# Writing each group of split weights at its own offset of 0 to 112 bytes inside the SBUF buffers

## The chip, the cores and the metric

One core of one Trainium2 chip runs the kernel. The metric is the device time in microseconds (us) of one execution; several executions are made and the median is compared.

## The reference

A trunk of two layers on 256 tokens of width 1024, in float32. Each layer is a half-step SwiGLU feed-forward block, a token-mixing block and a second feed-forward block, each followed by a layer norm:

```python
x = layer_norm(ALPHA * x + 0.5 * swiglu(x, ffn1_gate, ffn1_up, ffn1_down), ln1_g, ln1_b)
proj = x @ w_in                       # 1024 -> 2328 columns, for three mixers
mix = concat([short_conv(...), gmlp_spatial(...), nsa_attention(...)]) @ w_out
x = layer_norm(ALPHA * x + mix, ln2_g, ln2_b)
x = layer_norm(ALPHA * x + 0.5 * swiglu(x, ffn2_gate, ffn2_up, ffn2_down), ln3_g, ln3_b)

def swiglu(x, w_gate, w_up, w_down):  # 1024 -> 2816 -> 1024
    return (silu(x @ w_gate) * (x @ w_up)) @ w_down
```

## The kernel before

**Products in three passes.** Every large product is made of float32r matmuls. A float32 matrix is split in two float32r matrices, `hi` (the value rounded) and `lo` (what is left), and a product is hi*hi + hi*lo + lo*hi. So each pair of tiles costs three matmuls, each with a weight load of its own (in the trace PE is the matmul row of TensorE and PEld its weight loads).

**The stream of weights.** `_plan` lists all weight blocks in the order of their use. `ensure` walks through the list: it loads a block of at most 1024 columns into a `raw` buffer (SP's queue, L159), ScalarE rounds it into a `hi` buffer (L162) and VectorE subtracts to get the `lo` buffer (L163). There are 5 raw, 12 hi and 12 lo buffers, used in turn; a buffer is written again once the matmuls that read it are done. `blocks` and `kslices` hand out the tiles of a group and call `ensure` six or seven blocks ahead. A group is all blocks with the same key: the gate, up or down weights of one chunk of the feed-forward block, or one column group of `w_in`. `index` holds the keys in order: 71 per layer, 142 in all.

**Three kinds of large product.** The operand that is loaded into the array is called stationary here, the one that streams through is called moving.

- Channel products (`proj_chan`, L195 to L197): stationary is a 128x128 piece of a weight buffer, moving are 256 columns of the transposed activations `xTh` or `xTl`. The gates and ups of chunks 1 to 9 (tiles `pg`, `pu`) and most of the input projection (`pc`) are made so.
- Token products (`mm3`, L185 to L187): stationary is a 128x128 piece of `xTh` or `xTl`, moving is the weight buffer, 512 columns in the gate and up of chunk 0 (`pg`, `pu`), 280 or 256 columns in the first two groups of the input projection (`pt`).
- Down and output products (also `mm3`): stationary is a piece of the hidden activations (`hTh`, `hTl`) or of the mixers' output (`mixh`, `mixl`), moving are 512 columns of the weight buffer (`y`, `yo`).

**Where the operands lie.** A buffer has one address, the same in all 128 partitions; it is counted in bytes here. In the built program the raw, hi and lo buffers begin at 43328, 63808 and 112960, and each next buffer of a kind lies 4096 bytes further. All of them begin 64 bytes after a multiple of 128. So do the buffers of `hTh`, `hTl`, and of `mixh`, `mixl` (which are taken from the hi and lo buffers). `xTh` (25472) and `xTl` (33664) begin at a multiple of 128. The pieces that the matmuls of 128, 256 and 512 columns take begin at multiples of 512 bytes from there, so they have the same place in a stretch of 128 bytes as the buffer; only the 280-column products take pieces at 0, 1120 and 2240 bytes.

The lines of the helper that all products of 512 and 280 columns go through, and of the channel products:

```python
            PE.matmul(o, lhsT=a[0], rhs=b[0], start=start, stop=False)         # L185
            PE.matmul(o, lhsT=a[0], rhs=b[1], start=False, stop=False)         # L186
            return PE.matmul(o, lhsT=a[1], rhs=b[0], start=False, stop=stop)   # L187
...
                    PE.matmul(p[:, b, :], lhsT=hi, rhs=xTh[:, k, :], start=k == 0, stop=False)       # L195
                    PE.matmul(p[:, b, :], lhsT=hi, rhs=xTl[:, k, :], start=False, stop=False)        # L196
                    PE.matmul(p[:, b, :], lhsT=lo, rhs=xTh[:, k, :], start=False, stop=k == KC - 1)  # L197
```

Of the kernel before, what the change touches and what calls it, by code (L numbers as in the profile page):

```python
# [8 lines left out]
F32R = mybir.dt.float32r  # L9
# [112 lines left out]
def _build(tc, A, out):  # L122
# [3 lines left out]
    with ExitStack() as es:  # L126
# [3 lines left out]
        hip = pool("hi", 12)  # L130
        lop = pool("lo", 12)
# [7 lines left out]
        index = {}  # L139
# [9 lines left out]
        def ensure(i):  # L149
            while len(loaded) <= min(i, len(plan) - 1):  # L150
                key, k, n, split, o = plan[len(loaded)]
                src = A["ws"][o:o + 128 * n].rearrange("(p c) -> p c", p=128)
                if not split:
                    raw = (hip, lop)[k % 2].tile([128, n], F32, name="w1", tag=("hi", "lo")[k % 2])
                    SP.dma_start(raw, src)
                    loaded.append((raw, None))
                    continue
                raw = rawp.tile([128, n], F32, name="raw", tag="raw")
                stream.append(SP.dma_start(raw, src))  # L159
                hi = hip.tile([128, n], F32R, name="hi", tag="hi")  # L160
                lo = lop.tile([128, n], F32R, name="lo", tag="lo")
                splits.append((ACT.copy(hi, raw),  # L162
                               DVE.tensor_tensor(lo, raw, hi.bitcast(F32), ALU.subtract)))  # L163
                loaded.append((hi, lo))

        def blocks(key, ahead=None):
            if ahead is None:
                ahead = 7 if len(key) == 4 else 6
            ids = index[key]
            ensure(ids[-1] + ahead)  # L170
            return [loaded[i] for i in ids]
# [56 lines left out]
        for h, n in ((0, 1), (1, 4)):  # L228
            with ExitStack() as order:
                for i in prev:  # L230
                    order.enter_context(tc.issue_after(i.ins))
                x_load(0, h)
                prev = to_xT(0, h)
            with ExitStack() as order:
                for i in prev:
                    order.enter_context(tc.issue_after(i.ins))
                ensure(n)
            prev = splits[-1]
        for h in range(2):
            x_load(1, h)  # L240
        ensure(7)

        def second_x(products):
# [554 lines left out]
```

## Time and profile before

| | us |
|---|---|
| median of 3 runs (993.42 to 995.68) | 993.79 |
| the profiled execution, its own time | 993.1 |
| its span, first to last instruction | 991.4 |
| PE busy in the span | 978.0 |
| PEld (weight loads) busy | 887.4 |
| DVE (VectorE) busy | 603.2 |
| ACT (ScalarE) busy | 468.4 |

The profiled execution lies 0.7 us below the median. Busy time counts an instruction from its start to its end; matmuls overlap, so the time that one matmul costs is the distance from its start to the start of the next, called the spacing here, and not its own duration. The profile gives the spacing by the start times of the timeline, or by the number of matmuls in a stretch.

### The profile page before, as it was taken

How to read it: one execution, taken by the hardware profiler on the slowest of the kernel's cores; microseconds unless marked ns; L12 is line 12 of the kernel's file. 1: busy time of each engine (PE TensorE's matmuls, PEld its weight loads, DVE VectorE, ACT ScalarE, POOL GpSimd, SP SyncE). 2: the span in 40 equal slices, each digit the busy share in tenths (PEclk: the TensorE clock that was granted, in tenths of full speed). 3: DMA queues.
4: the chain of work that ended last, by engine and by line, in shares of the span. 5: the costliest groups of instructions: out<-in, count | busy, mean ns of one | idle time of the engine just before them, and what ended most of it. 6: DMA issues, size and time to landing. Idle time of an engine off the chain costs nothing.

```text
span 991.4 us, 16634 instructions
## 1 busy us (share of the span) xinstructions
PE 978.0 (99%) x6824; PEld 887.4 (90%) x6828; DVE 603.2 (61%) x830; ACT 468.4 (47%) x658; POOL 19.7 (2%) x42
## 2 busy tenths in 40 slices
PE   7999999999999999999999999999999999999996
PEld 6999999899878899999889999998988789999995
DVE  6655455686769555455584545548678785545534
ACT  6644444256655444344354444434565663534420
POOL 1000000010000000000000000000000000000000
PEclk9999999999999999999999999999999999999998
DMA  8967565385226666556375766554642265755601
GB/s 284 331 241 237 171 198 187 105 309 160 87 86 194 231 213 194 189 189 205 94 231 195 255 205 202 196 157 168 237 149 85 86 229 198 253 190 184 205 16 42
DMA packets 53067, 183.17 MB, mean 185 GB/s; under 512 B 6656, under 2 KB 7168, under 8 KB 52992
## 3 DMA queue, kind: packets, MB, share of 16 engines
q1 hardware_dynamic: 52992, 182.12, 55.2%
q8 instruction: 53, 0.87, 0.4%
q14 instruction: 22, 0.18, 0.1%
HBM read 181.05 MB, written 1.05 MB: 184 GB/s over the span
## 4 chain that ended last, share of the span: by engine, by line
PE 99%; DMA 0%; DVE 0%; issue 0%; SPq 0%; DVEq 0%; ACT 0%
PE y L185 8%; PE y L187 8%; PE y L186 8%; PE pu L195 7%; PE pg L195 7%; PE pg L197 7%; PE pu L197 7%; PE pg L196 7%; PE pu L196 7%; PE pc L195 3%; PE pc L197 3%; PE pc L196 3%; PE pg L187 2%; PE yo L187 2%; PE yo L185 2%; PE pg L185 2%
## 5 line engine op out<-in xcount | busy, mean ns | idle before, releaser
L163 DVE TENSOR_TENSOR lo<-raw,hi 128x1024 fp32r<-128x1024 f32 (+2 forms) x326 | 389.9, 1203 | 283.1 <-ACT hi L162 267.3
L162 ACT CAST hi<-raw 128x1024 fp32r<-128x1024 f32 (+2 forms) x326 | 335.1, 1037 | 385.6 <-PE pu L196 153.6
L195 PE MATMUL pu<-xTh,hi 128*128 128x256 f32 x576 | 161.3, 280 | 0.0
L195 PE MATMUL pg<-xTh,hi 128*128 128x256 f32 x576 | 161.3, 280 | 0.0
L197 PE MATMUL pu<-xTh,lo 128*128 128x256 f32 x576 | 160.8, 279 | 0.0
L197 PE MATMUL pg<-xTh,lo 128*128 128x256 f32 x576 | 160.8, 279 | 0.0
L196 PE MATMUL pu<-xTl,hi 128*128 128x256 f32 x576 | 160.8, 279 | 0.0
L196 PE MATMUL pg<-xTl,hi 128*128 128x256 f32 x576 | 160.7, 279 | 0.0
L185 PE MATMUL y<-hi,hTh 128*128 128x512 f32 x352 | 138.6, 394 | 0.0
L187 PE MATMUL y<-hi,hTl 128*128 128x512 f32 x352 | 137.4, 390 | 0.0
L186 PE MATMUL y<-lo,hTh 128*128 128x512 f32 x352 | 136.9, 389 | 0.0
L195 PEld LDWEIGHTS pu<-xTh,hi 128*128 128x128 f32 x576 | 108.1, 188 | 1.1
L196 PEld LDWEIGHTS pu<-xTl,hi 128*128 128x128 f32 x576 | 107.8, 187 | 1.1
L197 PEld LDWEIGHTS pu<-xTh,lo 128*128 128x128 f32 x576 | 108.3, 188 | 0.0
L197 PEld LDWEIGHTS pg<-xTh,lo 128*128 128x128 f32 x576 | 108.3, 188 | 0.0
L195 PEld LDWEIGHTS pg<-xTh,hi 128*128 128x128 f32 x576 | 108.1, 188 | 0.1
L196 PEld LDWEIGHTS pg<-xTl,hi 128*128 128x128 f32 x576 | 107.8, 187 | 0.1
L187 PEld LDWEIGHTS y<-hi,hTl 128*128 128x128 f32 x352 | 66.0, 188 | 14.7
L186 PEld LDWEIGHTS y<-lo,hTh 128*128 128x128 f32 x352 | 66.1, 188 | 12.6
L185 PEld LDWEIGHTS y<-hi,hTh 128*128 128x128 f32 x352 | 66.1, 188 | 12.3
L195 PE MATMUL pc<-xTh,hi 128*128 128x256 f32 x256 | 73.0, 285 | 0.0
L197 PE MATMUL pc<-xTh,lo 128*128 128x256 f32 x256 | 72.5, 283 | 0.0
(153 smaller groups left out, 1246.4 us busy)
## 6 DMA issues: line engine op xcount, KB each, us to landing
raw<-in_ws SPq DMA_DIRECT2D x312, 512.0 KB, 4.6
w<-in_ws SPq DMA_DIRECT2D x8, 512.0 KB, 6.1
lng<-in_ln SPq DMA_DIRECT2D x6, 512.0 KB, 6.7
lnb<-in_ln SPq DMA_DIRECT2D x6, 512.0 KB, 7.5
raw<-in_ws SPq DMA_DIRECT2D x8, 256.0 KB, 4.0
raw<-in_ws SPq DMA_DIRECT2D x4, 420.0 KB, 3.5
x<-in_x SPq DMA_DIRECT2D x4, 256.0 KB, 4.5
out<-x SPq DMA_DIRECT2D x4, 256.0 KB, 2.1
```

Source lines behind the costliest of these rows:

```text
L162: splits.append((ACT.copy(hi, raw), DVE.tensor_tensor(lo, raw, hi.bitcast(F32), ALU.subtract)))
L163: DVE.tensor_tensor(lo, raw, hi.bitcast(F32), ALU.subtract)))
L185: PE.matmul(o, lhsT=a[0], rhs=b[0], start=start, stop=False)
L186: PE.matmul(o, lhsT=a[0], rhs=b[1], start=False, stop=False)
L187: return PE.matmul(o, lhsT=a[1], rhs=b[0], start=False, stop=stop)
L195: PE.matmul(p[:, b, :], lhsT=hi, rhs=xTh[:, k, :], start=k == 0, stop=False)
L196: PE.matmul(p[:, b, :], lhsT=hi, rhs=xTl[:, k, :], start=False, stop=False)
L197: PE.matmul(p[:, b, :], lhsT=lo, rhs=xTh[:, k, :], start=False, stop=k == KC - 1)
```

## The change

Each group gets a number, its place in the list of keys modulo 8. The group's hi and lo parts are written into their buffers 4 elements (16 bytes) times that number behind the buffer's begin. To make room each hi and lo buffer grows from 1024 to 1056 elements, 4096 to 4224 bytes.

```diff
-                hi = hip.tile([128, n], F32R, name="hi", tag="hi")
-                lo = lop.tile([128, n], F32R, name="lo", tag="lo")
+                at = 4 * (list(index).index(key) % 8)
+                hi = hip.tile([128, 1056], F32R, name="hi", tag="hi")[:, at:at + n]
+                lo = lop.tile([128, 1056], F32R, name="lo", tag="lo")[:, at:at + n]
```

Everything that reads `hi` and `lo` goes through these slices. The other tiles that are taken from the same buffers (`KH`, `KL`, `QS`, `mixh`, `mixl`, the tile `w1`) stay at the buffer's begin, and the raw buffers are as before. In the built program the hi buffers now begin at 63808 and every 4224 bytes after it, the lo buffers at 114496 and every 4224; all still 64 bytes after a multiple of 128. The tiles allocated behind them move up by 3072 bytes, which is 24 times 128. `xTh` and `xTl` stay. The instructions of all five engines, their order, their shapes and what they wait for are the same in the two built programs. Of the 72 groups of channel products in the feed-forward blocks 8 have the number 0, and 8 to 11 each other number; of the 40 down groups 4 have the number 0.

## Rows read from the trace of the kernel before

**Rows 1.** The page: span, busy share of the engines, granted clock by fortieths, chain.
```profile
span 991.4 us, 16634 instructions
...
PE 978.0 (99%) x6824; PEld 887.4 (90%) x6828; DVE 603.2 (61%) x830; ACT 468.4 (47%) x658; POOL 19.7 (2%) x42
...
PEclk9999999999999999999999999999999999999998
...
PE 99%; DMA 0%; DVE 0%; issue 0%; SPq 0%; DVEq 0%; ACT 0%
```

**Rows 2.** Groups of PE, shapes apart: busy us, mean ns of one.
```profile
L195 PE MATMUL pu<-xTh,hi 128*128 128x256 f32 x576 | 161.3, 280 | 0.0
...
L185 PE MATMUL y<-hi,hTh 128*128 128x512 f32 x352 | 138.6, 394 | 0.0
...
L195 PE MATMUL pc<-xTh,hi 128*128 128x256 f32 x256 | 73.0, 285 | 0.0
...
L185 PE MATMUL yo<-hi,mixh 128*128 128x512 f32 x64 | 26.5, 414 | 0.0
L185 PE MATMUL pg<-hi,xTh 128*128 128x512 f32 x64 | 26.2, 409 | 0.0
```

**Rows 3.** Busy time by stretch: from:to, length, busy (instructions) of each engine, clock, DMA.
```profile
156.04:161.69 5.65, 5.65 (x50) 5.65 (x49) 2.45 (x3) 2.59 (x3) 0.00 (x0) 1.00 0.47 141
714.46:720.11 5.65, 5.65 (x50) 5.65 (x49) 4.55 (x6) 5.33 (x7) 0.00 (x0) 1.00 0.25 82
226.81:232.25 5.44, 5.44 (x51) 5.44 (x50) 4.35 (x6) 5.12 (x7) 0.00 (x0) 1.00 0.21 59
175.76:189.36 13.60, 13.60 (x62) 11.26 (x60) 6.00 (x11) 0.00 (x0) 0.92 (x1) 1.00 0.15 47
321.27:326.17 4.90, 4.90 (x23) 3.93 (x22) 2.74 (x3) 2.61 (x3) 0.00 (x0) 1.00 0.38 111
345.00:350.00 5.00, 5.00 (x45) 5.00 (x44) 0.11 (x1) 1.05 (x1) 0.00 (x0) 1.00 0.02 8
```

**Rows 4.** The same view for `pc` on PE alone: stretches with the closer spacing, and all.
```profile
208.70:237.70 29.00, 27.95 (x240) 1.00 0.66 221
696.14:707.10 10.96, 10.96 (x96) 1.00 0.89 313
0.00:991.40 991.40, 98.72 (x768) 1.00 0.56 185
```

**Rows 5.** Timeline of PE: L185 of four successive 280-column triples (start, duration).
```profile
202.84 0.29 PE L185 MATMUL pt<-hi,xTh 128*128 128x280 f32 x1
...
203.22 0.29 PE L185 MATMUL pt<-hi,xTh 128*128 128x280 f32 x1
...
203.62 0.29 PE L185 MATMUL pt<-hi,xTh 128*128 128x280 f32 x1
...
204.00 0.29 PE L185 MATMUL pt<-hi,xTh 128*128 128x280 f32 x1
```

**Rows 6.** Groups of DVE and ACT: the splits, and the shifted convolution taps.
```profile
L163 DVE TENSOR_TENSOR lo<-raw,hi 128x1024 fp32r<-128x1024 f32 x312 | 379.1, 1222 | 271.6 <-ACT hi L162 255.7 <-DMA w<-in_w 11.3
...
L478 DVE SCALAR_TENSOR_TENSOR vg<-vg,rs,gln 128x256 f32<-128x256 f32 x4 | 1.9, 481 | 0.9 <-POOL rs L302 0.9
L596 DVE SCALAR_TENSOR_TENSOR yc<-z,taps,yc 128x254 f32<-128x254 f32 x4 | 1.9, 480 | 0.1
```

**Rows 7.** Groups of ACT: the rounding of the weights.
```profile
L162 ACT CAST hi<-raw 128x1024 fp32r<-128x1024 f32 x312 | 325.5, 1052 | 373.3 <-PE pu L196 153.6 <-PE pg L196 78.5 <-PE y L187 54.7
```

**Rows 8.** Busy time by stretch, DVE alone, in the attention of the first layer.
```profile
242.00:275.00 33.00, 26.56 (x76) 1.00 0.30 97
275.00:309.00 34.00, 27.04 (x59) 1.00 0.35 104
```

## The prediction

> **What bounds the kernel now.** I read the page first. PE is busy for 978.0 of 991.4 us, the chain that ended last is PE to 99%, and the granted clock is at full speed in all slices but the last [rows 1]. So nothing but the pace of the matmuls sets the time, and the question about any change is whether it alters that pace or makes PE wait. The groups by line give counts and durations: a channel product of 256 columns lasts 280 ns, a down product of 512 columns 394 ns [rows 2]. They overlap, so these are not what one costs.
>
> For the cost I took the busy time by stretch, with stretches that run from the start of one L195 or L185 to the start of another, so that the code gives the number of products in them; the counts in the row are two or three higher, since they include matmuls that had begun before the stretch. The reader is to see four paces [rows 3]:
>
> - Channel products in the feed-forward block: 48 in 5.65 us, 117.7 ns each.
> - The same channel products in the input projection (`ks` and the first half of `q`): in the second layer, from 714.46, 48 in 5.65 us, 117.7 ns; in the first, from 226.81, 48 in 5.44 us, 113.3 ns.
> - Down products: 60 in 13.60 us, 226.7 ns, exactly twice 113.3.
> - Token products of 512 columns: 21 in 4.90 us, 233.3 ns.
>
> So a product of the same width has two paces, a close one (113.3 for 256 columns, 226.7 for 512) and a wide one (117.7 and 233.3). It is not other engines that make the difference: from 345 to 350 DVE is busy for 0.11 us, ACT for 1.05 us, the DMA share is 0.02, and about 43 channel products are still made in 5 us, at the wide pace [rows 3]. It isn't the granted clock either, which is 1.00 in all these rows. What is left is PE itself: the reading of the moving operand, and of the stationary operand of the next product, which goes on beside it. In the down products, at the close pace, both operands begin 64 bytes after a multiple of 128. In the token products one begins at 0 and the other at 64, in the channel products also, and there the wide pace rules. That fits a collision of the two reads that depends on where the operands lie. But place is not all: in the input projection of the first layer the channel products run close with the same places.
>
> **The change part by part.** No instruction is added, removed or moved on any engine, SP's queue of loads included. What changes are addresses, and with them three things.
>
> First, the writes of ACT and DVE into shifted buffers (L162, L163). Their prices are 1052 and 1222 ns per 1024 columns [rows 6, 7]. The nearest rows for a shift are the convolution taps: an operation with operands shifted by 4 and 8 bytes and 254 columns takes 480 ns, the like one without a shift and with 256 columns 481 [rows 6]. I take nothing. Were it a tenth more, it would be hidden: ACT is idle for 373.3 us before these roundings, most of it waiting for PE to free a buffer [rows 7], so the splits run ahead of their use. The cover is thinnest in the attention, where DVE is busy for 26.56 of 33 us and 27.04 of 34 [rows 8]; 6 to 7 us are free in each, and a tenth of the splits there, about twenty, would be 2.4 us. So between 0 and nothing that shows.
>
> Second, the place of the weights against the activations, which by the reading above chooses the pace. I count what can move:
>
> - Channel products at the wide pace: 6 groups of 576 in the feed-forward blocks [rows 2] are 3456; of the 768 of the input projection 240 and 96 lie in the close stretches [rows 4], so 432 are wide. Together 3888, each with 117.7 less 113.3, 4.4 ns, to gain: 17.1 us at most.
> - Token products of 512 columns: 6 groups of 64 [rows 2], 384, with 233.3 less 226.7, 6.6 ns: 2.5 us to gain at most.
> - Down and output products: 3 times 352 and 3 times 64 [rows 2], 1248, now close, with 6.6 ns to lose: 8.2 us at most.
>
> A group with the number 0 stays as it is, so seven eighths of these. No row shows a shift of 16, 32 or 48 bytes between the operands. The ends are therefore that all shifted groups are wide, and that all are close. I take the middle, that half of the new places give the close pace and half the wide one, for this reason: of the two relations that the rows show (0 and 64 bytes apart), one is close throughout and the other nearly always wide, so neither end has the rows on its side. That gives 7/8 of (-8.6 - 1.3 + 4.1), which is -5.1 us.
>
> Third, a moving operand that does not begin on a round place may be read more slowly in itself. The nearest rows are the 280-column products, whose pieces begin 64, 32 and 0 bytes after a multiple of 128: their triples take 0.38, 0.40 and 0.38 us [rows 5]. So at most 4%, on one of them. The down, output and token products are 1248 and 384 with some 228 ns, 372 us together; 4% of that on seven eighths is +13 us. I take 0, since the same place comes again later in the projection without standing out, and keep 13 for the range.
>
> **Sum.** 993.1 - 5.1 is 988.0 us for an execution like the profiled one, and as that lay 0.7 us below the median, 988.7 for the median, which I round to 989.
>
> **The rivals.**
>
> *The place does not matter.* The two paces may be set by how the stream of matmuls was entered, not by addresses: the same code with the same places runs at 113.3 in one layer and 117.7 in the other [rows 3], and it changes after small matmuls stand between. Against it: down and token products are the same helper, the same width, the same hi, lo, hi order, and differ in the stationary operand alone, and each keeps its pace throughout. Time: 993.8, within 2 us.
> The Trainium skill bears on this one: "TensorE: Matmul & The Clock Gate", in its section on what each phase is for, has two independent read ports in PE, one for each operand, so that loading the next weights takes no bandwidth from the running matmul; by that rule no place could matter and the sum would be 0. The trace agrees in that PE's pace is the same with all other engines at rest; that there are two paces for one width it doesn't explain, and so I leave it the smaller chance.
>
> *The down products lose and the gates don't gain.* This is the one on the other side. Down products have the close pace because their operands stand alike; every shift breaks that. If only the relation of 0 bytes is close, all shifted down and output products go to 233.3 ns, +7.2 us (7/8 of 8.2), while the channel products, of which only a group with the number 4 would come to stand alike, gain an eighth of 17.1, 2.1 us, or nothing if their pace is set by how they were entered. Time: 999 to 1001. It decides from the point where the share of down products that go wide is more than 2.4 times the share of channel and token products that go close (19.6 against 8.2 us). For it: 0 bytes is the one relation that is close in all its rows. Against it: a collision that needs the two reads to meet should be the exception among eight places.
>
> *Reading from a shifted place is slow in itself*, the third item above: up to +13 us, 1006.8; it decides if the cost is over 1.5% of the 372 us. For it is the one triple of 0.40 us [rows 5], against it that the others at that place differ little.
>
> *Nearly every shift is close*: 7/8 of -19.6, -17.2 us, 976.6. For it is the same thought about collisions; it is the far end of the forecast and shares its chance.
>
> That the change would not do what it says can be left out: the built program has the slices at the new addresses, and all readers use them.
>
> **How the numbers follow.** A measurement of this kernel tells about 0.2%, 2 us, from no change. The forecast with its far end (faster by 2 to 17 us) gets 0.45; no matter of place, or gains and losses that cancel, 0.23; the loss of the down products 0.20 and slow reading 0.12, together 0.32 for slower. The sum rests on a middle that no row shows, so the forecast's own range is wide, 977 to 991.7. The whole range goes from 976, all shifts close, to 1004, which takes in the loss of all down products and a part of the slow reading.
>
> **What would show it.** Right: in the profile after, stretches of channel products of different groups have different paces by their number, many at 113 ns, and some down groups are at 233; the mean durations of the L195 to L197 groups of `pg` and `pu` fall from 280 towards 276, those of `y` rise. No matter of place: all rows keep their counts and means. The loss of the down products: `y` rises with `pg`, `pu` unchanged. Slow reading: `y` and the 512-column `pg` beyond 234 ns. Wrong in another way: PE shows idle time before L185 or L195 with DVE or ACT as the releaser, or the DVE and ACT means of L162, L163 rise by tens of ns.

## The result, and the profile after

The changed kernel takes 1001.8 us (median of 4 runs, 1000.19 to 1002.69), the kernel before 993.93 in the same comparison. The ratio is 1.0077, with a 95% interval of 1.0059 to 1.0094. The change makes the kernel slower, where a gain of 5 us was forecast. The profiled execution took 1001.12 us, 999.4 of them its span. (L162, L163, L185 to L187 and L195 to L197 of before are L163, L164, L186 to L188 and L196 to L198 now.)

The page of the changed kernel: span, busy time, granted clock, the chain, and the PE groups that answer to [rows 1, 2].

```profile
span 999.4 us, 16638 instructions
...
PE 985.9 (99%) x6828; PEld 891.1 (89%) x6828; DVE 603.2 (60%) x830; ACT 468.0 (47%) x658; POOL 19.3 (2%) x42
...
PEclk9999999999999999999999999999999999999999
...
PE 98%; DMA 0%; DVE 0%; SPq 0%; issue 0%; DVEq 0%; ACT 0%
...
L196 PE MATMUL pg<-xTh,hi 128*128 128x256 f32 x576 | 161.7, 281 | 0.0
...
L186 PE MATMUL y<-hi,hTh 128*128 128x512 f32 x352 | 139.7, 397 | 0.0
```

Its groups with the shapes apart: the splits on DVE and ACT, as [rows 6, 7], and further groups of PE, as [rows 2].

```profile
L164 DVE TENSOR_TENSOR lo<-raw,hi 128x1024 fp32r<-128x1024 f32 x312 | 378.8, 1222 | 276.4 <-ACT hi L163 275.3
...
L163 ACT CAST hi<-raw 128x1024 fp32r<-128x1024 f32 x312 | 325.0, 1050 | 378.1 <-PE pu L197 160.9 <-PE pg L197 82.3 <-PE y L188 57.0
...
L196 PE MATMUL pc<-xTh,hi 128*128 128x256 f32 x256 | 73.7, 288 | 0.0
...
L186 PE MATMUL pg<-hi,xTh 128*128 128x512 f32 x64 | 25.9, 405 | 0.0
```

PE is busy 7.9 us longer and the span is 8.0 us longer; what PE idles, 999.4 less 985.9, is 13.5 us, and was 13.4. So no wait was added: the matmuls themselves go at another pace, at the full clock. The writes kept their means, 1222 and 1050 ns. The durations say where the time is only roughly: 281 for 280 ns in the gates, 397 for 394 in `y`, 288 for 285 in `pc`, 405 for 409 in the token products. The cost is read from the spacing again.

Busy time by stretch of the changed kernel, PE alone (from:to, length, busy and count, clock, DMA share, GB/s). Each of the first six stretches holds 48 channel products of one group, the seventh 78 down products, the last 24 token products. The groups' numbers are 0, 0, 0, 4, 5 and 6.

```profile
114.73:120.22 5.49, 5.49 (x49) 1.00 0.66 226
406.62:412.08 5.46, 5.46 (x51) 1.00 0.47 162
151.35:156.96 5.61, 5.61 (x51) 1.00 0.69 227
168.27:173.98 5.71, 5.71 (x50) 1.00 0.68 208
389.68:395.38 5.70, 5.70 (x50) 1.00 0.49 142
145.69:151.35 5.66, 5.66 (x49) 1.00 0.85 287
173.98:192.09 18.11, 18.11 (x81) 1.00 0.19 59
311.91:317.50 5.59, 5.59 (x26) 1.00 0.89 301
```

The paces now differ by the group's number. The number 0 has 114.4, 113.8 and 116.9 ns, so it is close for a part of its products; but the number 4, whose weights stand like `xTh` modulo 128 (both begins leave the same rest), has 119.0, the number 5 118.8, and the number 6 117.9. Before, such a stretch took 117.7 [rows 3]. The down products have 232.2 ns, for 226.7 before [rows 3]. The token products, 232.9, are nearly as they were.

The same over the whole execution, each spacing taken from the start times and summed: the channel products of the feed-forward blocks (3456) took 407.2 us before and 408.5 now, `pc` 94.2 and 95.9, the token products 92.4 and 91.8, `y` 241.4 and 246.1, `yo` 48.2 and 48.5, and the 256-column `pt` took 0.2 us more. That is +1.3, +1.7, -0.6, +4.7, +0.3 and +0.2, before rounding together 7.7 of the 7.9 us by which PE is longer busy. By number, and without the few spacings above 150 ns, the channel products have 115.6 (0), 117.7, 117.5, 119.0, 119.1 (4), 118.5, 119.4 and 118.0 ns (7). The 119.4 of the number 6 comes mostly from one group, in which 28 of the 48 products are 130 to 134 ns apart. Its busy time by stretch, PE alone:

```profile
844.71:850.82 6.11, 6.11 (x51) 1.00 0.61 186
```

That is 127.3 ns for a channel product, at the full clock. e3, below, has the same spacings in the same group. `y`, without spacings above 245 ns, has 231.7 to 233.4 in all numbers, and that holds for the number 0 as well (232.1), which the change was to leave as it is.

That last number calls for a second cause: the growth of the buffers. Before, all hi and lo buffers begin 64 bytes after a multiple of 256. With 4224 bytes from one to the next every second one begins 192 bytes after it. (The built programs mostly take the buffers in turn, but not always, so that successive blocks mostly alternate between the two places.) The prediction looked at places modulo 128 only, where this can't be seen.

### The profile page after: what moved, and what is told of

It reads as the page before. It is cut to its first block, busy times and chain, and to the rows that moved or that the text cites. A ratio compares the mean times of both kernels' runs of the same rounds, so it can differ in the third digit from the quotient of the medians.

```text
span 999.4 us, 16638 instructions
## 1 busy us (share of the span) xinstructions
PE 985.9 (99%) x6828; PEld 891.1 (89%) x6828; DVE 603.2 (60%) x830; ACT 468.0 (47%) x658; POOL 19.3 (2%) x42
## 4 chain that ended last, share of the span: by engine, by line
PE 98%; DMA 0%; DVE 0%; SPq 0%; issue 0%; DVEq 0%; ACT 0%
PE y L188 8%; PE y L187 8%; PE y L186 8%; PE pu L196 7%; PE pg L197 7%; PE pu L198 7%; PE pu L197 7%; PE pg L198 7%; PE pg L196 7%; PE pc L196 3%; PE pc L198 3%; PE pc L197 3%; PE yo L187 2%; PE yo L186 2%; PE yo L188 2%; PE pg L187 2%
## 5 line engine op out<-in xcount | busy, mean ns | idle before, releaser
L164 DVE TENSOR_TENSOR lo<-raw,hi 128x1024 fp32r<-128x1024 f32 (+2 forms) x326 | 389.7, 1203 | 288.0 <-ACT hi L163 286.8
L163 ACT CAST hi<-raw 128x1024 fp32r<-128x1024 f32 (+2 forms) x326 | 334.6, 1035 | 390.4 <-PE pu L197 160.9
L196 PE MATMUL pg<-xTh,hi 128*128 128x256 f32 x576 | 161.7, 281 | 0.0
L198 PE MATMUL pu<-xTh,lo 128*128 128x256 f32 x576 | 161.7, 281 | 0.0
L197 PE MATMUL pg<-xTl,hi 128*128 128x256 f32 x576 | 161.7, 281 | 0.0
L197 PE MATMUL pu<-xTl,hi 128*128 128x256 f32 x576 | 161.6, 281 | 0.0
L196 PE MATMUL pu<-xTh,hi 128*128 128x256 f32 x576 | 161.6, 281 | 0.0
L198 PE MATMUL pg<-xTh,lo 128*128 128x256 f32 x576 | 161.6, 281 | 0.0
L186 PE MATMUL y<-hi,hTh 128*128 128x512 f32 x352 | 139.7, 397 | 0.0
L188 PE MATMUL y<-hi,hTl 128*128 128x512 f32 x352 | 139.0, 395 | 0.0
L187 PE MATMUL y<-lo,hTh 128*128 128x512 f32 x352 | 138.8, 394 | 0.0
L196 PEld LDWEIGHTS pu<-xTh,hi 128*128 128x128 f32 x576 | 108.5, 188 | 1.3
L197 PEld LDWEIGHTS pu<-xTl,hi 128*128 128x128 f32 x576 | 108.4, 188 | 1.2
L197 PEld LDWEIGHTS pg<-xTl,hi 128*128 128x128 f32 x576 | 108.5, 188 | 0.1
L196 PEld LDWEIGHTS pg<-xTh,hi 128*128 128x128 f32 x576 | 108.5, 188 | 0.1
L198 PEld LDWEIGHTS pg<-xTh,lo 128*128 128x128 f32 x576 | 108.6, 188 | 0.0
L198 PEld LDWEIGHTS pu<-xTh,lo 128*128 128x128 f32 x576 | 108.6, 188 | 0.0
L188 PEld LDWEIGHTS y<-hi,hTl 128*128 128x128 f32 x352 | 66.1, 188 | 15.6
L187 PEld LDWEIGHTS y<-lo,hTh 128*128 128x128 f32 x352 | 66.2, 188 | 14.1
L186 PEld LDWEIGHTS y<-hi,hTh 128*128 128x128 f32 x352 | 66.2, 188 | 13.9
L196 PE MATMUL pc<-xTh,hi 128*128 128x256 f32 x256 | 73.7, 288 | 0.0
L198 PE MATMUL pc<-xTh,lo 128*128 128x256 f32 x256 | 73.1, 286 | 0.0
```

Of the source, the lines that this page charges most:

```text
L163: splits.append((ACT.copy(hi, raw), DVE.tensor_tensor(lo, raw, hi.bitcast(F32), ALU.subtract)))
```

## The experiments

The theories are told in the quoted expectations. A minus in a diff marks a line of the changed kernel; e4 to e7 start from the kernel before, and e12 from e11. The ratios are to the kernel before in the same comparison. The table gives for each kernel its median, and the mean spacing in ns of the channel products in the feed-forward blocks, of the token products without spacings over 245 ns, and of `y`, all from the start times of the profiled execution.

| kernel | us | channel | token | y |
|---|---|---|---|---|
| before | 993.93 | 117.8 | 233.4 | 228.8 |
| the change | 1001.8 | 118.2 | 232.0 | 233.3 |
| e1 bigger buffers alone | 986.97 | 115.1 | 231.4 | 231.8 |
| e2 offsets for moving weights only | 985.03 | 114.3 | 232.0 | 233.2 |
| e3 offsets for stationary weights only | 999.52 | 118.2 | 231.4 | 231.6 |
| e4 all moved by 64 bytes | 1001.69 | 120.0 | 227.6 | 228.5 |
| e5 all moved by 128 | 990.7 | 117.6 | 229.7 | 227.8 |
| e6 all moved by 256 | 994.27 | 117.8 | 233.3 | 228.8 |
| e7 all moved by 32 | 990.84 | 116.7 | 233.2 | 228.4 |
| e8 buffers of 4352 bytes alone | 994.04 | 117.8 | 233.3 | 228.8 |
| e9 these, with the change's offsets | 1000.11 | 118.1 | 233.2 | 232.2 |
| e10 these, offsets for stationary only | 997.72 | 118.5 | 233.3 | 228.8 |
| e11 these, every second block 128 further | 980.15 | 114.1 | 233.3 | 228.6 |
| e12 as e11, token weights 64 further | 977.92 | 114.1 | 227.8 | 228.6 |

### The two parts of the change (e1, e2, e3)

e1 keeps the bigger buffers and drops the offsets:

```diff
-                at = 4 * (list(index).index(key) % 8)
+                at = 0
```

> Buffers of 1056 elements (4224 bytes) as in the change, but every group at the buffer's begin. Theory A (the place of the weights within a stretch of 128 bytes decides; the offsets are the cause): as before, 994 us within 2, down products at 227 to 228 ns, channel products at 117.8. Theory B (the distance of 4224 bytes from buffer to buffer is the cause, as it ends the common place of all buffers within 512 and 1024 bytes): down products at 231 to 233 ns (+4.5 us), channel products at about 115.6 ns as the groups of number 0 have in the changed kernel (-7.6 us), 989 to 993 us.

e2 keeps the offsets of those weights that are the moving operand (down and output weights, chunk 0, the first two groups of the input projection), e3 those of the others:

```diff
+                moves = key[1] in ('kvg', 'v', 'wo') or len(key) == 4 and (key[2] == 'd' or key[3] == 0)
-                at = 4 * (list(index).index(key) % 8)
+                at = 4 * (list(index).index(key) % 8) * moves
```

In e3 the last factor is `(not moves)`.

> Offsets only for the groups whose weights are the moving operand (down, output projection, chunk 0, first two of the input projection); the others at the buffer's begin, all buffers of 4224 bytes. Theory A: down products 232 to 233 ns, channel products 117.8 as before, 999 to 1000 us. Theory B: down products 232 to 233 ns, channel products about 115.6 ns, 990 to 994 us.

> Offsets only for the groups whose weights are the stationary operand (channel products); down and token groups at the buffer's begin, all buffers of 4224 bytes. Theory A: down products 227 to 228 ns, channel products 118.0 to 118.2, 995 to 996 us. Theory B: down products 231 to 232 ns, channel products 118.0 to 118.2, 1000 to 1001 us.

Measured: e1 986.97 us, ratio 0.9932 [0.9915, 0.9949]; e2 985.03, 0.9911 [0.9895, 0.9928]; e3 999.52, 1.0058 [1.0040, 1.0076].

The bigger buffers alone, which no term of the prediction held, make the kernel 6.6 us faster. The offsets of the stationary weights then cost 12.6 us (e3 against e1) or 16.8 (the change against e2); those of the moving weights gain 1.9 us (e2 against e1), but not in the products that they move: `y` goes from 231.8 to 233.2 ns, the channel products from 115.1 to 114.3. So the change is a gain that it gives away twice over. Both e1 and e2 lie below the range that either theory gave them. What e1 does to the two kinds of product stands in its busy time by stretch, PE alone: two successive groups of 48 channel products, 48 of the second feed-forward block, and 78 down products.

```profile
45.35:50.95 5.60, 5.60 (x49) 1.00 0.82 300
50.95:56.39 5.44, 5.44 (x50) 1.00 0.53 123
343.65:349.31 5.66, 5.66 (x50) 1.00 0.04 12
171.91:189.96 18.05, 18.05 (x81) 1.00 0.18 59
```

These are 116.7, 113.3 and 117.9 ns for a channel product, with no offset anywhere, and 231.4 for a down product, where before had 226.7. In the first group the first 36 products go at 118 and the last twelve at 113.4, and the close pace stays until the next down products. In the built program the blocks of the first two groups alternate between 64 and 192 bytes; in the third group all weights lie at 64, and it stays wide.

### All weights moved against the activations (e4 to e7)

A small tile behind `xTl` moves everything that is allocated after it, all weight buffers and the hidden activations among it, against `xTh` and `xTl`, in the kernel before. Nothing else changes:

```diff
         xTl = cst.tile([128, KC, S], F32R, name="xTl")
+        cst.tile([128, 16], F32, name="pad")
```

16 elements are 64 bytes (e4), 32 are 128 (e5), 64 are 256 (e6), 8 are 32 (e7). In e4 weights and `xTh` stand alike modulo 256, both at 128; the two operands of `y` stand alike in all four.

> The kernel before, with 64 bytes left free behind the transposed activations, so that all weight buffers and the hidden activations move by 64 bytes together and stand like the transposed activations within 512 bytes; buffers 4096 bytes apart. Theory A, with the equal place as the close one: down products stay at 227 to 228 ns, channel products go from 117.8 to 113.3 and token products from 233.3 to 226.7, 975 to 977 us. Rival, after the rows of the changed kernel in which the channel operands stand a multiple of 128 bytes apart (118.6 to 119.6 ns): channel products at about 119.5 ns, +6 us, 1000 us. If places don't matter at all: 994 us.

Measured: e4 1001.69 us, ratio 1.0077 [1.0059, 1.0096]. Its busy time by stretch, PE alone: 48 channel products, 36 down products, 48 token products.

```profile
49.28:55.04 5.76, 5.76 (x50) 1.00 0.58 162
55.04:63.23 8.19, 8.19 (x38) 1.00 0.97 321
20.55:31.44 10.89, 10.89 (x50) 1.00 0.97 334
```

The token products went from 233.3 to 226.9 ns in this stretch, as the prediction's reading (standing alike is close) wants it. The channel products did the opposite, 120.0 ns, the widest mean of the table, and constant. The same relation of places gives the close pace for 512 columns and one wider than any of before for 256. This run alone refutes the step by which the prediction carried the rule from `y` to the gates; and it shows that the place decides, since nothing but addresses differs from before and 8 us are lost. For 512 columns it is the place of one operand against the other: `y` keeps 227.8 to 228.8 ns in e4 to e7, where both of its operands move together.

> The kernel before with 128 bytes left free behind the transposed activations: weights and hidden activations move together, buffers 4096 bytes apart, the stationary weights still 64 bytes off within 128 but 448 instead of 64 bytes off within 512. Theory C (the place within 256 or 512 bytes chooses between the close and the wide pace; in the kernel with buffers of 4224 bytes and no offsets the distances other than 64 ran at 113.3 to 115): channel products at 113.3 to 115, down products stay at 227 to 228, 976 to 983 us. Theory D (only the place within 128 bytes counts, and the wide pace of the kernel before comes from all its buffers standing alike): channel products at 117.8, 993 to 994 us.

> The same with 256 bytes: 320 instead of 64 bytes off within 512, equal to before within 256. Theory C with 512 bytes as the measure: 113.3 to 115 ns, 976 to 983 us; with 256 bytes as the measure, and theory D: 117.8 ns, 993 to 994 us. Down products at 227 to 228 ns in each case.

> The same with 32 bytes: every stationary weight 32 bytes nearer, as in the groups with the number 2 of the changed kernel, but alike for all buffers. If the distance from 64 modulo 128 is what costs the channel products: about 117.5 ns as those groups have, 992 to 994 us, and it may not have a close state at all; if it is the mixture of places that costs, 113.3, 976. Down products at 227 to 228 ns.

Measured: e5 990.7 us, ratio 0.9957 [0.9940, 0.9973]; e6 994.27, 0.9995 [0.9986, 1.0005]; e7 990.84, 0.9960 [0.9945, 0.9975].

A shift by 256 bytes changes neither the time nor, by more than 0.1 ns, a spacing of the table, one by 128 does (token products 229.7 for 233.4): for these shifts the place counts modulo 256. e7 has neither pace of before in its channel products. They go at 116.7 ns, nearly constant; 48 of them in its busy time by stretch, PE alone:

```profile
50.92:56.52 5.60, 5.60 (x50) 1.00 0.52 157
```

e5, by contrast, shows two paces with one set of places. Its busy time by stretch, PE alone: the first 48 channel products, ahead of all down products, 48 after the first down products, and 36 down products.

```profile
32.11:37.65 5.54, 5.54 (x52) 1.00 0.93 325
...
49.22:54.87 5.65, 5.65 (x51) 1.00 0.50 146
54.87:63.03 8.16, 8.16 (x39) 1.00 0.98 337
```

The first are 115.4 ns on average and 113.3 at their end; from the first down products to the end of the block, all channel products take 117.7, and the other feed-forward blocks repeat it, their first group close and the rest wide. So where weights stand 64 bytes off from `xTh`, a pace is kept once it is entered, and in e5 the down products leave PE in the wide one. e5's time, 990.7 us, lies between the ranges of the two theories. This answers only a part of the question that the prediction left open, why the same places ran close in one layer and wide in the other [rows 3]: both paces can hold with one set of places, but between the close products of the second layer [rows 4] and the wide ones behind them (those from 714.46 in [rows 3] among them) stand no down products, only small matmuls, as in the first layer. What made the switch there isn't shown.

### Buffers that keep their place modulo 256 (e8, e9, e10)

Buffers of 1088 elements, 4352 bytes, all begin 64 bytes after a multiple of 256, as before. e8 has no offsets (`at = 0`), e9 those of the change, e10 those of the stationary weights alone (the line of e3):

```diff
-                hi = hip.tile([128, 1056], F32R, name="hi", tag="hi")[:, at:at + n]
-                lo = lop.tile([128, 1056], F32R, name="lo", tag="lo")[:, at:at + n]
+                hi = hip.tile([128, 1088], F32R, name="hi", tag="hi")[:, at:at + n]
+                lo = lop.tile([128, 1088], F32R, name="lo", tag="lo")[:, at:at + n]
```

> Buffers of 1088 elements, 4352 bytes apart (a multiple of 256), every group at the begin. Theory E (the place within 256 bytes decides; a shift by 256 of everything left all as it was): as before, down products 227 to 228 ns, channel products 117.8, 993 to 995 us. Theory F (any growth of the buffers breaks the common place, since it has a longer period): like the kernel with 4224 bytes and no offsets, down at 231, channel products at 115, 987 us.

> The change's offsets for all groups, in buffers 4352 bytes apart. Theory E: the offsets alone cost; channel products of number 0 at 113 to 118, of the other numbers 117 to 119.5, mean 118; down products of number 0 at 227 to 229, the others 231 to 234, mean 232; 1000 to 1002 us. Theory F: the same as the change, 1001.8 us, with the down products of number 0 at 232 as well.

> Offsets for the groups with stationary weights alone, buffers 4352 bytes apart, down and token groups at the begin. Theory E: down products 227 to 228 ns as before, channel products 118 to 118.3, 995 to 997 us. Theory F: down products 231 ns, 1000 us.

Measured: e8 994.04 us, ratio 1.0005 [0.9995, 1.0015]; e9 1000.11, 1.0067 [1.0052, 1.0082]; e10 997.72, 1.0041 [1.0026, 1.0056].

e8 is the kernel before in every spacing of the table, to 0.1 ns: it is not the size of the buffers that gave e1 its gain but their alternating place. With that out of the way the offsets cost 6.1 us, 3.7 by the stationary weights (e10 against e8) and 2.4 by the moving ones (e9 against e10). In e9 the place of each group is known from its number alone. Its busy time by stretch, PE alone: 48 channel products of the number 4, then two neighbours in one sequence of `y`, 12 products of the number 0 and 12 of the number 3.

```profile
88.05:93.80 5.75, 5.75 (x51) 1.00 0.67 189
481.33:484.05 2.72, 2.72 (x14) 1.00 0.77 277
484.05:486.85 2.80, 2.80 (x14) 1.00 0.12 48
```

The number 4 takes 119.8 ns in the channel products: it is e4's relation, and e4's pace. The down products take 226.7 ns with the number 0 and 233.3 with the number 3. Over all of e9, `y` without spacings above 245 ns goes at 228.5 (0), 231.4, 232.9, 233.2, 229.1 (4), 231.1, 233.5 and 229.0 (7), and the channel products, without those above 150 ns, at 115.6 (0), 116.7, 117.1, 118.7, 119.8 (4), 118.3, 118.2 and 119.3 (7). In two of the eight groups of the number 7 the spacing alternates between some 117 and 130 ns, through nearly all 48 products; the other six have 117.8 to 118.4 ns. One of the two, PE alone:

```profile
354.52:360.43 5.91, 5.91 (x51) 1.00 0.55 166
```

That is 123.1 ns, and e10 has the same pace in four groups of this number. So e4's 120.0 is not the widest that a place can give.

### A place that alternates on purpose (e11, e12)

If a step of the place by 128 bytes frees the channel products from the wide pace, it can be had without the loss in the down products: only the stationary weights alternate, in buffers that keep their place.

```diff
-                at = 4 * (list(index).index(key) % 8)
+                moves = key[1] in ('kvg', 'v', 'wo') or len(key) == 4 and (key[2] == 'd' or key[3] == 0)
+                at = 32 * (len(loaded) % 2) * (not moves)
```

The buffers are those of e8.

> Buffers 4352 bytes apart; of the groups with stationary weights every second block stands 128 bytes further, all other groups at the begin. Theory E with the place's jump as what frees the channel products from the wide pace: down products stay at 227 to 228 ns, channel products run at 113.3 from the second jump after a down product on, mean 114.3 to 115.1, 979 to 983 us, faster than both kernels. If the close pace in the kernel with 4224 bytes came from the down products before them being out of step: channel products 117.8, 994 us.

Measured: 980.15 us (978.59 to 980.55), ratio 0.9860 [0.9846, 0.9875]. Its busy time by stretch, PE alone: 24 down products, then the first 12 channel products, the next 36, and the next group of 48.

```profile
74.96:80.43 5.47, 5.47 (x27) 1.00 0.68 224
80.43:81.84 1.41, 1.41 (x13) 1.00 0.95 314
81.84:85.92 4.08, 4.08 (x38) 1.00 0.91 292
85.92:91.36 5.44, 5.44 (x50) 1.00 0.58 192
```

The down products keep their pace (227.9). The first 12 channel products, all at 64 bytes, go at 117.5; the first block at 192 bytes is the step, and from there it is 113.3, through 36 products with two more steps and through the whole next group. In the second feed-forward block the first 12 channel products after the down products stand at 192 bytes and the next 12 at 64; three stretches of 12, PE alone:

```profile
341.70:343.12 1.42, 1.42 (x13) 1.00 0.12 49
343.12:344.54 1.42, 1.42 (x15) 1.00 0.04 12
344.54:345.90 1.36, 1.36 (x15) 1.00 0.00 0
```

The step from 192 to 64 leaves them at some 118 ns; the step back to 192 brings 113.3. So it is in the feed-forward blocks of all of e11, by the start times: all 29 steps from 64 to 192 that meet the wide pace end it, none of the 14 from 192 to 64 does. Against e8 nothing differs but these steps, and 13.9 us are gained.

e12 besides moves the gate and up weights of chunk 0 to the place of `xTh`, the relation in which e4's token products were close:

```diff
-                at = 32 * (len(loaded) % 2) * (not moves)
+                at = 16 if moves and len(key) == 4 and key[2] in 'gu' else 32 * (len(loaded) % 2) * (not moves)
```

> The kernel with buffers of 4352 bytes and every second stationary block 128 bytes further, and besides the gate and up weights of chunk 0 (moving, 512 columns) written 64 bytes behind the buffer's begin, where they stand like xTh and xTl modulo 256. Theory E (products of 512 columns are close when both operands stand alike modulo 256): the 384 token products go from 233.3 to about 227.5 ns, the value they had with everything shifted by 64 bytes, so 2.2 us less than the 980.15 measured without this edit, about 978; channel products stay at 114 and y at 228.6. Rival G (the token products were close in that earlier run because what ran before them had changed too, not by their own place): token products stay at 233.3 and the time at 980. A side effect could be that the channel products after chunk 0 are entered in the wide state for longer: then pg and pu of chunk 1 go above 114 and the time stays at 980 or more with token products at 227.5.

Measured: 977.92 us (977.69 to 978.64), ratio 0.9836 [0.9823, 0.9849]. Busy time by stretch of e12, PE alone, 48 token products:

```profile
21.70:32.59 10.89, 10.89 (x49) 1.00 0.94 331
```

The same 48 in e11:

```profile
21.90:33.09 11.19, 11.19 (x49) 1.00 0.93 339
```

226.9 for 233.1 ns; rival G falls. e12 is 2.2 us faster than e11, of which the 384 token products make 2.1 (227.8 for 233.3 ns). It is 16 us faster than the kernel before and 24 us faster than the change.

## Why the prediction was wrong

**What bounds the kernel** was right: PE's pace alone, in every run (the chain that ended last is PE to 96 to 99% in all of them). That the two paces come from where the operands lie was right as well; the rival that the place does not matter falls with e4, which moves addresses only and loses 8 us. Its other half, that a pace goes by how the stream of matmuls was entered, holds for the channel products beside the place (e5). By the Trainium skill's rule of two read ports ("TensorE: Matmul & The Clock Gate", its section on what each phase is for), as the rival read it, no place could matter. As a statement on the time it does not hold here: the measured spacings, 113.3 to 120.0 ns for one and the same product, decide against it. Which of the reads is in the way no run shows.

**The writes** were priced at 0, and that held: 1222 and 1050 ns, as in [rows 6, 7]. **No wait was added**, as forecast. **Slow reading** of a moving operand was priced at 0 with 13 us kept in the range; no number's `y` in the changed kernel goes above 233.4 ns on average (without spacings above 245 ns), so nothing of that shows beyond the wide pace.

**The channel term is the step that failed**: "I take the middle, that half of the new places give the close pace and half the wide one". It gave 7/8 of -8.6, -7.5 us. Measured was +1.3 us in the feed-forward blocks and +1.7 in `pc`, +3.0. None of the seven new places has the close pace on average; in e9 they have 116.7 to 119.8 ns, mostly wider than the wide one. That is 10.5 of the 12.8 us between 989 and 1001.8. Two things led there. The prediction treated all products as having the same rule, close when the operands stand alike, and so read the gates' wide pace as the loss of a place that a shift could restore (it looked at places modulo 128, by which the number 4 would stand alike); e4 shows that for 256 columns this place is worse than that of before. And it knew only two paces, so that a new place could gain 4.4 ns or nothing, but not lose. The number 4, named as the one that "would come to stand alike", was the slowest in e9 (119.8 ns).

**The down and output term** was of the right sign, and too small: +3.6 us forecast, +5.0 measured (4.7 and 0.3). The middle was too kind here: 5.0 of the 7.2 us of the rival were lost, and part of it not through the offsets but through the bigger buffers, which take the close pace from the number 0 too (e1: 231.8 ns with no offsets, e8: 228.8).

**The token term** was of the right sign: 7/8 of -1.3, -1.1 us, forecast, -0.6 measured.

**The growth of the buffers** had no term. The text noted that all buffers still begin 64 bytes after a multiple of 128 and went on. By e1 it is worth -6.6 us when it stands alone, because the alternating place frees channel products; under the offsets this gain cannot be seen.

**The rival on the other side**, down products lose and the gates don't gain, is what happened in its direction, with 999 to 1001 us for 1001.8 measured. That the number comes so near is partly luck: its down part was too large by some 2 us and its channel part too hopeful by 3 to 5, and the two make up for each other. Its point of decision, a share of wide down products over 2.4 times the share of close channel products, was passed, since the channel products lost on the whole. The argument held against it, that a collision should be the exception among eight places, was turned round by the runs for the channel products, where the close pace is the exception; for `y` in e9 the numbers 4 and 7 (229.1 and 229.0 ns) come near the number 0 (228.5).

What stays open: why the place has this effect. A collision between the reading of the moving operand and that of the next stationary one would fit, but is only argued. `xTh` stands at the same place in all kernels, so for the channel products the runs don't tell whether it is the distance from `xTh` that counts or the weights' own place; for 512 columns they do. Why one place gives two paces, among them the 130 ns of the number 7, is open too. Why the down products leave the channel products in the wide pace, and why not every step of the place frees them, was not settled either: in e11 each step of both parts from 64 to 192 bytes after down products did, in e1 the first step of hi and lo from 64 to 192 bytes after down products mostly did nothing and the second freed them, and in its second feed-forward block such a step left the wide pace at 402.7 us and ended it at 450.5.

## What to carry to other kernels

Where PE is the bound, compare the spacing of like products by stretch before looking for work to remove; two paces of the same product, with the other engines at rest, point to where the operands lie, and a pad tile of some tens of bytes is the cheapest way to test it. A change of places should be tried on each kind of product for itself and with the buffers' step, modulo 256, kept apart from the offset: here a rule found on 512 columns had the opposite sign on 256, and the buffers' step alone moved more time than was forecast for the whole change.

## What was not expected of the hardware

- The place of the operands counts modulo 256 bytes, as far as tried: moved by 256, every spacing is the same to 0.1 ns (e6), and so it is with buffers 17 times 256 bytes apart (e8); moved by 128, the token products go from 233.4 to 229.7 ns (e5).
- For 512 columns, operands that stand alike give 226.7 to 228.5 ns; a moving operand 64 bytes ahead of the stationary one 229 to 230 (e5's token products, e9's number 4), one 112 ahead 229.0 (e9's number 7), one 64 behind 233.3 (the token products of before), the other places mostly 231 to 233.5.
- For 256 columns alike gives a constant 120.0 ns (e4), 32 bytes off a nearly constant 116.7 (e7), and 64 bytes off has two paces that each keep themselves up, 113.3 and 117.8 (e5). 48 bytes off has two as well, some 118 ns and one that alternates between 117 and 130 (e9 and e10). A step of both parts of the weights from 64 to 192 bytes changes from the wide to the close one (in e11, where the step from 192 to 64 does not; in e1 not each time), and it stays through later steps until down products come between (e11).
